# Keys, cached keys, convolution state and parameters in the kernel's own layout in DRAM

## The chip, the cores and the metric

The kernel runs on one core of one Trainium2 chip. The metric is the device time of one execution in microseconds; the time before is the median of three runs. The engines are named as in the profile: PE is TensorE, DVE is VectorE, ACT is ScalarE, POOL is GpSimd, and SP issues most transfers (ACT and POOL can issue transfers too).

## What is computed

The reference is one step of a streaming encoder: one trunk layer over 1024 prompt rows and 32 sample rows, 1056 rows in all, of width 1024. Cut to what matters here:

```
h = rmsnorm(x, g_mix) * (1 + sc1) + sh1          # sc1, sh1, ... from silu(c) @ w_ada + b_ada
u = h @ w_in
qa, ka, va, qm, km, vm, om, ip, fp, ga, gm = split(u)
ya = band_attention(qa, ka, va, rel_bias)        # 8 heads x 64; sample rows also see cache_k, cache_v
new_k, new_v = ka[:, T - keep:], va[:, T - keep:]  # the prompt's last 512 rows; all 32 sample rows
xpad = concatenate([conv_left, concatenate([qm, km])])
conv = sum(xpad[:, j:j + T] * conv_w[j] for j in range(4)) + conv_b
new_conv = xpad[:, -3:]
ym = mlstm(silu(conv), vm, ip, fp, C, n, m)      # 4 heads x 128
merged = sigmoid(ga) * (ya @ w_br_att) + sigmoid(gm) * (ym @ w_br_mlstm)
x = x + gt1 * (merged @ w_out)                   # then a gated feed-forward layer and a last rmsnorm
```

All of it is float32. The new keys and values, the last three rows ahead of the convolution and the mLSTM state are outputs beside y.

## The kernel before, in words

Activations stand with their features on the 128 partitions and the 1056 rows along the free axis, in three tiles of 352 rows. A float32 product is made of three matmuls: each operand is split into a high part (made by ACT) and a low part (made by DVE or POOL), and high x high, low x high and high x low are summed. So a product of 128 output features with a depth of 1024, called a unit, is 8 x 3 = 24 matmuls of 352 columns into one buffer "mm" (`unit`, matmuls at L458). A weight block of 1024 x 128 has three units. SP loads it (`wraw`, L434), ACT and DVE or POOL split it (`wsp`, L424 and L425); `W.advance()` decides when the next ones are loaded and split, in the order of a list.

The program starts with the layer's input, the adaLN products and the norm; then come the first K and V blocks of `w_in`. Attention goes by pairs of heads, `hp` = 0 to 3, each with a K, a V and a Q block. The attention of a pair is made while the products of the next pair run: a generator is stepped by the units. Its steps are scores (psS, L747), bias and maximum (L761 on DVE), exponential (L762 on ACT), normalising (L767 on POOL), transposes of the scores (psT, L774), their split (L781 on ACT, L786 on DVE) and the product with V (psV, L805). In the fourth pair's attention the units beside it are those of the mLSTM's gates and products (L906). The remaining adaLN products run on DVE in between (L1227, L1229), on weights `wa` that SP loads at L1216.

PE transposes whatever has rows on the partitions in DRAM: the small parameters (L239), the cached keys (L700), the convolution state (L860), the keys and the last rows of the convolution on their way out (L582, L587, L1323), and the values (L631), which the kernel itself needs with rows on the partitions. Parameters are loaded by eight transfers into rows of 128 and copied by DVE (L240). After a K block the float32 keys of the last 512 prompt rows and the 32 sample rows stand in `kf` (written by ACT at L571). `k_tail` transposes them in four pieces, ACT copies them (L595) and issues the store itself (L596); `sample_tail` does the same with 32 rows, with a copy by DVE (L589) and a store by SP (L590).

These tails are side work. A K block appends three entries to a list `side.later`: nothing, `k_tail`, `sample_tail`. A V block appends `v_tail` for the first half of the rows, nothing, `v_tail` for the second half, nothing, and `v_sample`, and in the first pair `cache_kv`, which splits the cached keys and values. `unit` takes one entry off this list behind its third, fifth and seventh group of three matmuls. `v_tail` transposes four pieces of the float32 values that ACT copied at L606 and splits them (L619 on ACT, L622 on DVE); the second one also stores them, through L595 and L596.

Every engine works off its instructions in the program's order. A transfer counts its end on one of eight lanes (DMAHW0 to DMAHW7) that are used in turn; an instruction that uses a lane again first waits until the lane's earlier transfer has landed. `q_block` (units of Q) copies each finished unit out of its buffer by ACT (L659, L662).

Of the kernel before, what the change touches and what calls it, by code (L numbers as in the profile page):

```python
# [139 lines left out]
def hybrid_stream_step(  # L140
    ctx: ExitStack,
    tc: tile.TileContext,
    x_prompt, x_sample, cache_k, cache_v, state_conv, state_C, state_n, state_m,
    c_prompt, c_sample, w_ada, b_ada, g_mix, w_in, b_if, conv_w, conv_b, rel_row,
    mh_gain, w_br_att, w_br_mlstm, w_out, g_ffn, w_gate_up, w_down, g_final,
    y_prompt, y_sample, new_k_p, new_v_p, new_conv_p, new_C_p, new_n_p, new_m_p,
# [49 lines left out]
    def f(ap):  # L196
        return ap.bitcast(F32)
# [361 lines left out]
    def k_block(hp):  # L559
        w = w_cols(KA + hp * P)  # L560

        def run():
# [11 lines left out]
            W.advance()  # L574
            side.later += [lambda: None, lambda: k_tail(hp, kf), lambda: sample_tail(kf[:, 512:], new_k_s, hp)]
        run.w = w
        return run

    def k_tail(hp, kf):
        pt = mmt()  # L580
        for i in range(4):
            pe.transpose(pt[:, i * P:(i + 1) * P], kf[:, i * P:(i + 1) * P], ident)  # L582
        put_tokens(pt, new_k_p, hp)

# [102 lines left out]
    def cache_loads():  # L687
        ckv = tmpt((P, 2, 512))
        sp.dma_start(ckv[:, 0], cache_k[0, 0].rearrange("t h d -> t (h d)"))
        sp.dma_start(ckv[:, 1], cache_v[0, 0].rearrange("t h d -> t (h d)"))  # L690
        sp.dma_start(rb_d, bass.AP(rel_row.tensor, rel_row.offset, [[FLEN, H], [0, P], [1, FLEN]]))
        return ckv

    def cache_kv(ckv):
        t = slot([P, 2, 2, 512], F32R)
        cv = t[:, 0].rearrange("p s c -> p (s c)").rearrange("p (h s d) -> p h s d", s=2, d=DH)
        ck = t[:, 1].rearrange("p s (g t) -> p s g t", g=4)
        pt = mmt()
        for g in range(4):
            pe.transpose(pt[:, g * P:(g + 1) * P], ckv[:, 0, g * P:(g + 1) * P], ident)  # L700
# [154 lines left out]
    def conv_state():  # L855
        sp.dma_start(tri[:24], state_conv[0, 0].rearrange("j (r c) -> (j r) c", c=P))

    def mlstm_setup():
        pt = mmt()
        pe.transpose(pt[:, :24], tri[:24], ident[:24, :24])  # L860
        dve.tensor_copy(scol, pt[:, :24])
        pool.memset(tri, 1.0)
# [1372 lines left out]
    for j in range(KD):  # L2235
# [19 lines left out]
        for c, a, b in col_segments(cut, T):  # L2255
# [6 lines left out]


_INS = ["x_prompt", "x_sample", "cache_k", "cache_v", "state_conv", "state_C", "state_n", "state_m",
        "c_prompt", "c_sample", "w_ada", "b_ada", "g_mix", "w_in", "b_if", "conv_w", "conv_b", "rel_bias",
        "mh_gain", "w_br_att", "w_br_mlstm", "w_out", "g_ffn", "w_gate_up", "w_down", "g_final"]
_KV = (1, 1, 512, H, DH)
_OUTS = [(1, S, D), (1, TS, D), _KV, _KV, (1, 1, 3, D), (1, 1, MH, P, P), (1, 1, MH, P), (1, 1, MH),
         (1, 1, TS, H, DH), (1, 1, TS, H, DH), (1, 1, 3, D), (1, 1, MH, P, P), (1, 1, MH, P), (1, 1, MH)]

# [24 lines left out]
```

## Time and profile before

| | us |
|---|---|
| median of three runs | 1608.19 |
| the three runs | 1606.87, 1608.19, 1608.39 |
| the profiled execution's own span | 1604.4 |
| outside the span (median less span) | 3.8 |
| PE busy in the profiled execution | 1576.2 |

The profiled execution has no time of its own but its span, from the first instruction to the last; the runs' times include what lies around it. Rows of the timeline give the start in us from the span's start, the duration, the engine, the line and the operation, what is written and read, how many instructions the row holds, and in brackets the idle time ahead of it with what ended it. A row of PE gives the length of its matmuls with their pipeline, so rows overlap; the starts tell the pace. A wait for several things is put down to the one that came last.

### The profile page before, as it was taken

Reading aid. Unit: us, or ns where it says so; the run is one execution under the profiler, and the core shown is the slowest. Engines: PE = TensorE matmul, PEld = TensorE weight load, DVE = VectorE, ACT = ScalarE, POOL = GpSimd, SP = SyncE. Lnnn points to the kernel's source line nnn. Section 1 sums busy time; section 2 is a strip of 40 time slices with the busy share of each in tenths; the row PEclk is TensorE's granted clock in tenths of the full one; section 3 lists DMA queues with packets and bytes.
Section 4 is the critical chain, followed back from the end, with each engine's and each line's share of the span. In section 5 each row is a group of like instructions: output and inputs, shape, how many; then the busy total and the mean of one; then the engine's idle time right before and its main releaser. Section 6 shows DMA issues by size and latency. Waiting matters only on the chain.

```text
span 1604.4 us, 27406 instructions
## 1 busy us (share of the span) xinstructions
PE 1576.2 (98%) x10256; PEld 1554.8 (97%) x10256; DVE 1135.5 (71%) x2185; ACT 786.2 (49%) x1747; POOL 445.3 (28%) x477
## 2 busy tenths in 40 slices
PE   7999999999999999999999999999999999999997
PEld 6989999999999999999999999999999999999997
DVE  7766564646776855556654699988888986799754
ACT  3665463544455644444443655554544444545443
POOL 2344243433332411000012100566565650000001
PEclk9999999999999999999999999999999999999999
DMA  9823323232222232675353311313222227427453
GB/s 362 273 77 91 97 82 102 88 122 86 67 80 80 69 95 69 121 276 168 121 153 113 106 54 48 100 55 105 81 79 94 67 82 252 135 79 250 135 156 126
DMA packets 210414, 192.45 MB, mean 120 GB/s; under 512 B 10706, under 2 KB 180618, under 8 KB 209258
## 3 DMA queue, kind: packets, MB, share of 16 engines
q1 hardware_dynamic: 205386, 187.82, 37.4%
q10 hardware_dynamic: 4640, 2.82, 0.6%
q8 instruction: 81, 1.33, 0.4%
q14 instruction: 51, 0.42, 0.1%
q0 software_dynamic: 256, 0.06, 0.0%
HBM read 152.19 MB, written 41.63 MB: 121 GB/s over the span
## 4 chain that ended last, share of the span: by engine, by line
PE 88%; DVE 5%; DMA 3%; ACT 2%; issue 1%; SPq 0%; ACTq 0%; POOL 0%; DVEq 0%; POOLq 0%
PE mm L458 39%; PE psb L1843 18%; PE mm L1843 10%; PE mm L2246 3%; PE mm L906 3%; PE psb L2246 2%; PE psV L805 2%; PE psb L2089 2%; PE psS L747 1%; DMA s<-in_w_ada_dram 1%; PE psT L774 1%; PE mm L2089 1%; DMA wraw<-in_w_in_dram 1%; DMA t<-in_x_sample_dram 1%; DVE s L390 1%
## 5 line engine op out<-in xcount | busy, mean ns | idle before, releaser
L458 PE MATMUL mm<-s,wsp 128*128 128x352 f32 x4104 | 689.1, 324 | 0.0
L458 PEld LDWEIGHTS mm<-s,wsp 128*128 128x128 f32 x4104 | 656.9, 188 | 2.0 <-issue 0.4
L425 DVE TENSOR_TENSOR wsp<-wraw,wsp 128x512 fp32r<-128x512 f32 (+1 forms) x280 | 234.9, 855 | 120.0 <-ACT wsp L424 118.0
L1843 PE MATMUL psb<-s,wsp 128*128 128x352 f32 x1611 | 271.7, 322 | 1.5 <-DVE wsp L425 0.8
L424 ACT ACTIVATE wsp<-wraw 128x512 fp32r<-128x512 f32 x336 | 199.5, 617 | 141.5 <-PE psb L1843 44.0
L1843 PEld LDWEIGHTS psb<-s,wsp 128*128 128x128 f32 x1611 | 260.6, 188 | 2.1 <-DVE wsp L425 1.1
L1843 PE MATMUL mm<-s,wsp 128*128 128x352 f32 x933 | 159.3, 322 | 0.0
L1843 PEld LDWEIGHTS mm<-s,wsp 128*128 128x128 f32 x933 | 151.2, 188 | 0.5 <-DVE wsp L425 0.5
L767 POOL TENSOR_SCALAR st<-st,mx 128x640 f32<-128x640 f32 (+5 forms) x72 | 55.7, 774 | 184.8 <-DVE mx L766 170.5
L1229 DVE SCALAR_TENSOR_TENSOR t<-wa,cmix,t 128x512 f32<-128x512 f32 x112 | 89.1, 801 | 15.0 <-DMA wa<-in_w_ada_dram 14.6
L425 POOL TENSOR_TENSOR wsp<-wraw,wsp 128x512 fp32r<-128x512 f32 x56 | 75.8, 1374 | 49.4 <-ACT wsp L424 47.9
L762 ACT ACTIVATE st<-st,mx 128x640 f32<-128x640 f32 (+5 forms) x72 | 47.9, 666 | 71.6 <-DVE mx L761 70.3
L761 DVE CUSTOM_DVE_ANT_0 st<-psS,bias 128x640 f32<-128x640 f32 (+5 forms) x72 | 44.3, 616 | 46.1 <-PE psS L747 33.2
L1790 POOL TENSOR_TENSOR t<-t,sl 128x352 f32<-128x352 f32 x19 | 18.3, 961 | 185.3 <-DMA wraw<-in_w_out_dram 130.8
L781 ACT ACTIVATE pT<-psT 128x640 fp32r<-128x640 f32 (+3 forms) x80 | 38.6, 493 | 63.1 <-PE psT L774 47.7
L2158 POOL TENSOR_TENSOR fst<-fst 128x1 f32<-128x1 f32 (+1 forms) x6 | 1.2, 192 | 236.6 <-ACT t L2151 236.6
L786 DVE TENSOR_TENSOR pT<-psT,pT 128x640 fp32r<-128x640 f32 (+3 forms) x80 | 43.9, 557 | 22.5 <-ACT pT L781 22.3
L1452 POOL TENSOR_TENSOR wraw<-wraw,raw 128x512 f32<-128x512 f32 x33 | 55.8, 1702 | 0.9
L906 PE MATMUL mm<-s,s 128*128 128x264 f32 (+3 forms) x432 | 54.8, 283 | 0.0
L2246 PE MATMUL mm<-s,wsp 128*128 128x352 f32 x330 | 54.4, 324 | 0.0
L2246 PEld LDWEIGHTS mm<-s,wsp 128*128 128x128 f32 x330 | 53.1, 188 | 0.0
L1452 POOL TENSOR_TENSOR spare<-wraw 128x512 f32<-128x512 f32 x11 | 16.5, 1496 | 130.0 <-DMA wraw<-in_w_gate_up_dram 122.4
(396 smaller groups left out, 2561.3 us busy)
## 6 DMA issues: line engine op xcount, KB each, us to landing
wraw<-in_w_in_dram SPq DMA_DIRECT2D x38, 512.0 KB, 4.0
wraw<-in_w_gate_up_dram SPq DMA_DIRECT2D x33, 512.0 KB, 3.8
wa<-in_w_ada_dram SPq DMA_DIRECT2D x64, 256.0 KB, 2.9
wraw<-in_w_down_dram SPq DMA_DIRECT2D x32, 512.0 KB, 4.0
a_d<-t SPq DMA_DIRECT2D x22, 528.0 KB, 2.8
g_d<-t SPq DMA_DIRECT2D x16, 528.0 KB, 3.9
x<-xres SPq DMA_DIRECT2D x16, 528.0 KB, 6.7
t<-g_d SPq DMA_DIRECT2D x16, 528.0 KB, 5.4
```

The lines of the kernel that those rows point to most:

```text
L424: act.activation(dst[:, 0], src, AF.Copy)
L425: eng.tensor_tensor(dst[:, 1], src, f(dst[:, 0]), op=ALU.subtract)
L458: pe.matmul(pt[:, :hi - lo], wt[(w0 + k) // 4][:, a, (w0 + k) % 4], xt[k][:, b, lo:hi], start=(k == 0 and q == 0), stop=(k == n - 1 and q ...
L761: dve.tensor_tensor_reduce(so, sv, bi, -1.0, 3.0e38, ALU.add, ALU.min, mx[:n, 1:2])
L762: act.activation(st[:n, :w], st[:n, :w], AF.Exp, bias=mx[:n, 1:2], scale=-1.0, accum_out=mx[:n, 2:3])
L767: pool.tensor_scalar(st[:n, :w], st[:n, :w], mx[:n, 3:4], 1.0, op0=ALU.mult, op1=ALU.mult)
L906: pe.matmul(pt[:n, :wd], hs[k][:, a, i * P:i * P + n], whl[b][:, k, :wd], start=(k == 0 and q == 0), stop=(k == KD - 1 and q == 2))
L1229: dve.scalar_tensor_tensor(ac[:, c], wa, cmix[:, c, k:k + 1], ac[:, c], op0=ALU.mult, op1=ALU.add)
L1452: self.eng.tensor_tensor(a(dst), a(x), a(y), op=op)
L1843: pe.matmul(acc, wt[:, a, k], x[k][:, b], start=(start and not onto and k == 0 and q == 0), stop=(stop and k == 3 and q == 2), skip_group_ ...
L2089: pe.matmul(acc, wt[k // 4][:, u, k % 4], piece_of[k, i][:, v], start=(k == 0 and q == 0), stop=(k == KP - 1 and q == 2))
L2246: pe.matmul(acc, wt[(k - k0) // 4][:, u, (k - k0) % 4], piece_of[k, 2][:, v], start=(k == 0 and q == 0), stop=(k == NF - 1 and q == 2))
```

## The change

The arrays are brought into the kernel's layout outside the kernel, or left in it: the eight small parameters come as one array `params` of 128 x 124, `cache_k` and `state_conv` come with the features on the partitions, and the new keys and the last rows of the convolution go out with the features on the partitions. The 27 transposes of these by PE, and the copies behind them, go. `v_tail` and `v_sample` stay. The core of the diff:

```diff
-    def param_loads():
-        for row, src in ((R_C, c_prompt), (R_C + 8, c_sample), (R_ADA, b_ada), (R_GMIX, g_mix), (R_GFFN, g_ffn),
-                         (R_GAIN, mh_gain), (R_CB, conv_b)):
-            pool.dma_start(prow[row:row + src.shape[-1] // P], src.rearrange("o (r c) -> (o r) c", c=P))
-        pool.dma_start(prow[R_CW:R_CW + 32], conv_w.rearrange("o j (r c) -> (o j r) c", c=P))
...
-    param_loads()
+    pool.dma_start(cols, params)
...
     def param_cols():
-        pt = ps_v()
-        pe.transpose(pt[:, :NR], prow[:NR], ident[:NR, :NR])
-        dve.tensor_copy(cols, pt[:, :NR])
...
             W.advance()
-            side.later += [lambda: None, lambda: k_tail(hp, kf), lambda: sample_tail(kf[:, 512:], new_k_s, hp)]
+            sp.dma_start(new_k_p[hp], kf[:, :512])
+            sp.dma_start(new_k_s[hp], kf[:, 512:])
...
-    def k_tail(hp, kf):
-        pt = mmt()
-        for i in range(4):
-            pe.transpose(pt[:, i * P:(i + 1) * P], kf[:, i * P:(i + 1) * P], ident)
-        put_tokens(pt, new_k_p, hp)
...
-        sp.dma_start(ckv[:, 0], cache_k[0, 0].rearrange("t h d -> t (h d)"))
+        sp.dma_start(ckv[:, 0], cache_k)
...
-        pt = mmt()
-        for g in range(4):
-            pe.transpose(pt[:, g * P:(g + 1) * P], ckv[:, 0, g * P:(g + 1) * P], ident)
-        pt4 = pt.rearrange("p (g t) -> p g t", g=4)
+        k4 = ckv[:, 0].rearrange("p (g t) -> p g t", g=4)
...
-            act.activation(ck[u, hh], pt4[u], AF.Copy)
+            act.activation(ck[u, hh], k4[u], AF.Copy)
...
-            dve.tensor_tensor(ck[v, hh], pt4[u], f(ck[u, hh]), op=ALU.subtract)
+            dve.tensor_tensor(ck[v, hh], k4[u], f(ck[u, hh]), op=ALU.subtract)
...
-        sp.dma_start(tri[:24], state_conv[0, 0].rearrange("j (r c) -> (j r) c", c=P))
+        sp.dma_start(scol, state_conv)
...
-        pt = mmt()
-        pe.transpose(pt[:, :24], tri[:24], ident[:24, :24])
-        dve.tensor_copy(scol, pt[:, :24])
...
-        pt = mmt()
-        pe.transpose(pt[:48, :P], ncv, ident)
-        ncr = tmpt((48, P))
-        dve.tensor_copy(ncr, pt[:48, :P])
-        sp.dma_start(new_conv_p[0, 0].rearrange("j (r c) -> (j r) c", c=P), ncr[0:24])
-        sp.dma_start(new_conv_s[0, 0].rearrange("j (r c) -> (j r) c", c=P), ncr[24:48])
+        for out, j in ((new_conv_p, 0), (new_conv_s, 3)):
+            sp.dma_start(out, ncv[:, j:j + 3])
```

Line numbers move with the change: L458, L631, L619, L595, L596, L659, L662, L434 and L1216 of the kernel before are L447, L615, L603, L579, L580, L643, L646, L423 and L1194 after. The order of the instructions shows what the shorter list does in the first q block. On PE before: `mm_738`, `mm_783` are the buffers of the first two units, `mm_754` and `mm_768` take the transposed keys, `mm_794` the first V tail.

```order
L458 MATMUL mm_738<-s_531,s_648 128x352 x3
L458 MATMUL mm_738<-s_558,s_648 128x352 x3
L458 MATMUL mm_738<-s_585,s_648 128x352 x3
L582 MATMUL mm_754<-ident,kf_700 128x128 [waits DVE_49,PE_49,Activation_49]
L582 MATMUL mm_754<-ident,kf_700 128x128 [waits Activation_49]
L582 MATMUL mm_754<-ident,kf_700 128x128 x2
L458 MATMUL mm_738<-s_611,s_648 128x352 x3
L458 MATMUL mm_738<-s_638,s_648 128x352 x3
L587 MATMUL mm_768<-ident,kf_700 32x128 [waits DVE_49]
L458 MATMUL mm_738<-s_675,s_648 128x352 x3
```

The same place on PE after: `mm_729` is the first unit, `mm_740` and `mm_759` take the two V tails, and `t_714` holds the values that ACT copies.

```order
L447 MATMUL mm_729<-s_486,s_637 128x352 x3
L447 MATMUL mm_729<-s_520,s_637 128x352 x3
L615 MATMUL mm_740<-ident,t_714 128x128 [waits DVE_49,Activation_49]
L615 MATMUL mm_740<-ident,t_714 128x128
L615 MATMUL mm_740<-ident,t_714 128x128 [waits Activation_49]
L615 MATMUL mm_740<-ident,t_714 128x128
L447 MATMUL mm_729<-s_547,s_637 128x352 x3
L447 MATMUL mm_729<-s_574,s_637 128x352 x3
L447 MATMUL mm_729<-s_600,s_637 128x352 x3
L447 MATMUL mm_729<-s_627,s_637 128x352 x3
L615 MATMUL mm_759<-ident,t_714 128x128 [waits DVE_49]
```

The K tail behind the fifth group and the sample tail behind the seventh are gone; the first V tail has come from the second unit to the first, behind the third group, and the second V tail to the place behind the seventh.

ACT in the same block, before: L595 and L596 copy and store the keys and later the values; L659 and L662 copy the unit `mm_738`, then `mm_783`.

```order
L595 ACTIVATE stg_759<-mm_754 128x512 [waits PE_49]
L596 DMA out_dram<-stg_759 128x4x128 [waits DMAHW4_49,Activation_49]
L659 ACTIVATE t_732<-mm_738 128x352 [waits PE_49]
L662 ACTIVATE s_731<-mm_738 64x352 [waits DVE_49,Pool_49]
L662 ACTIVATE s_731<-mm_738 64x352
L619 ACTIVATE s_793<-mm_794 128x8x64 [waits DMAHW0_49,PE_49]
L619 ACTIVATE s_793<-mm_813 128x8x64 [waits PE_49]
L595 ACTIVATE stg_820<-mm_813 128x512 [waits DMAHW4_49,DVE_49]
L596 DMA out_dram<-stg_820 128x4x128 [waits DMAHW6_49,Activation_49]
L659 ACTIVATE t_732<-mm_783 128x352 [waits PE_49]
```

And after: L603 is the split of the values, L579 and L580 copy and store them, L643 and L646 copy the unit `mm_729`, and L685 splits the cached keys in `t_715`.

```order
L603 ACTIVATE s_739<-mm_740 128x8x64 [waits DVE_49,PE_49,Pool_49]
L603 ACTIVATE s_739<-mm_759 128x8x64 [waits PE_49]
L579 ACTIVATE stg_766<-mm_759 128x512 [waits DVE_49]
L580 DMA out_dram<-stg_766 128x4x128 [waits DMAHW6_49,Activation_49]
L643 ACTIVATE t_723<-mm_729 128x352 [waits PE_49]
L646 ACTIVATE s_722<-mm_729 64x352 [waits DMAHW0_49]
L646 ACTIVATE s_722<-mm_729 64x352
L685 ACTIVATE s_809<-t_715 64x512 [waits DMAHW5_49,DMAHW2_49,DMAHW1_49]
```

The store of the values now stands ahead of the copies of the first unit, where it stood ahead of those of the second. PE's third unit waits for the copies of the first, whose buffer it takes.

The lane that this store waits for, DMAHW6, is held by another transfer, as SP's rows show. Before:

```order
L434 DMA wraw_721<-in_w_in_dram 128x8x128 [waits DMAHW7_49,DMAHW3_49,Pool_49]
L690 DMA t_724<-in_cache_v_dram 128x512 [waits DMAHW5_49]
L1216 DMA wa_733<-in_w_ada_dram 128x512 [waits DMAHW6_49]
L590 DMA out_dram<-stg_770 32x128 [waits DVE_49]
L1216 DMA wa_922<-in_w_ada_dram 128x512 [waits DMAHW0_49]
```

After, with `kf_689` the keys of the first pair:

```order
L423 DMA wraw_710<-in_w_in_dram 128x8x128 [waits DMAHW7_49,DMAHW3_49,Pool_49]
L565 DMA out_dram<-kf_689 128x32 [waits DMAHW4_49]
L673 DMA t_715<-in_cache_k_dram 128x512 [waits DMAHW5_49,PE_49]
L674 DMA t_715<-in_cache_v_dram 128x512 [waits DMAHW6_49]
L1194 DMA wa_724<-in_w_ada_dram 128x512
```

Lane 6 was that of an ada load and is now that of cache_v; cache_k, which stood ahead of the weight load `wraw_721`, now stands behind the same load and behind the sample keys.

In the fourth pair's attention SP's order before was:

```order
L832 DMA ya_d<-t_2920 128x1056 [waits DVE_49]
L678 DMA g_d<-t_3889 128x1056 [waits DMAHW0_49,Activation_49]
L434 DMA wraw_4046<-in_w_in_dram 128x8x128 [waits DMAHW1_49,Pool_49]
L1216 DMA wa_4075<-in_w_ada_dram 128x512 [waits DMAHW4_49,DMAHW2_49,DVE_49]
L1216 DMA wa_4137<-in_w_ada_dram 128x512 [waits DMAHW6_49,DMAHW3_49,DVE_49]
```

And after:

```order
L813 DMA ya_d<-t_2871 128x1056 [waits DVE_49]
L1194 DMA wa_4012<-in_w_ada_dram 128x512 [waits DMAHW4_49,DMAHW0_49,DVE_49]
L662 DMA g_d<-t_3829 128x1056 [waits DMAHW1_49,Activation_49]
L423 DMA wraw_3983<-in_w_in_dram 128x8x128 [waits DMAHW2_49,Pool_49]
L1194 DMA wa_4074<-in_w_ada_dram 128x512 [waits DMAHW6_49,DMAHW3_49,DVE_49]
```

One ada load has moved ahead of a gate store and a weight load. Elsewhere the engines' instructions keep their order, less those that went; the stores of the keys stand on SP ahead of the next weight load (L423), and the two stores of the convolution rows ahead of the ada loads near 560 us.

More of the change, by code (lines that the diff above doesn't have):

```diff
@@ L143, in hybrid_stream_step @@
     x_prompt, x_sample, cache_k, cache_v, state_conv, state_C, state_n, state_m,
-    c_prompt, c_sample, w_ada, b_ada, g_mix, w_in, b_if, conv_w, conv_b, rel_row,
-    mh_gain, w_br_att, w_br_mlstm, w_out, g_ffn, w_gate_up, w_down, g_final,
+    params, w_ada, w_in, b_if, rel_row, w_br_att, w_br_mlstm, w_out, w_gate_up, w_down, g_final,
     y_prompt, y_sample, new_k_p, new_v_p, new_conv_p, new_C_p, new_n_p, new_m_p,
@@ L210, in hybrid_stream_step @@
     pool.memset(ssq, 1.0)
-    prow = tmpt((P, P))
+    NR = R_C + 16
+    cols = cp.tile([P, NR], F32, name="cols")
     xtok = []
-    def param_loads():
-        for row, src in ((R_C, c_prompt), (R_C + 8, c_sample), (R_ADA, b_ada), (R_GMIX, g_mix), (R_GFFN, g_ffn),
-                         (R_GAIN, mh_gain), (R_CB, conv_b)):
-            pool.dma_start(prow[row:row + src.shape[-1] // P], src.rearrange("o (r c) -> (o r) c", c=P))
-        pool.dma_start(prow[R_CW:R_CW + 32], conv_w.rearrange("o j (r c) -> (o j r) c", c=P))
     for i in range(KD):
@@ L226, in hybrid_stream_step @@
         sp.dma_start(xtok[i], xp[i * P:(i + 1) * P])
-    param_loads()
+    pool.dma_start(cols, params)
     xsm = tmpt((TS, D))
     sp.dma_start(xsm, xs_in)
-    NR = R_C + 16
-    cols = cp.tile([P, NR], F32, name="cols")
     csil = cp.tile([P, KD, 2], F32, name="csil")
@@ L2261, in hybrid_stream_step @@
     mm_cm.__exit__(None, None, None)
+_PARAMS = ["b_ada", "g_mix", "g_ffn", "mh_gain", "conv_w", "conv_b", "c_prompt", "c_sample"]
 _INS = ["x_prompt", "x_sample", "cache_k", "cache_v", "state_conv", "state_C", "state_n", "state_m",
[L2265 to L2269, printed above, removed]
+        "params", "w_ada", "w_in", "b_if", "rel_bias",
+        "w_br_att", "w_br_mlstm", "w_out", "w_gate_up", "w_down", "g_final"]
+_V = (1, 1, 512, H, DH)
+_OUTS = [(1, S, D), (1, TS, D), (4, P, 512), _V, (P, 3, KD), (1, 1, MH, P, P), (1, 1, MH, P), (1, 1, MH),
+         (4, P, TS), (1, 1, TS, H, DH), (P, 3, KD), (1, 1, MH, P, P), (1, 1, MH, P), (1, 1, MH)]
 def kernel(**inputs):
@@ L2281 @@
     for name in _INS:
-        a = _np.asarray(inputs[name])
+        if name == "params":
+            a = _np.concatenate([_np.asarray(inputs[n]).reshape(-1, P) for n in _PARAMS]).T
+        else:
+            a = _np.asarray(inputs[name])
         if name == "rel_bias":
             a = _np.pad(a[0][:, ::-1], ((0, 0), (383, 64)), mode="edge")
+        if name == "cache_k":
+            a = a.reshape(P, 4, P).transpose(2, 1, 0).reshape(P, 512)
+        if name == "state_conv":
+            a = a.reshape(24, P).T
         a = _np.ascontiguousarray(a)
@@ L2293 @@
     r = _run(nc, [arrays], core_ids=[0])
-    return tuple(r.results[0][f"out_{i}_dram"] for i in range(len(_OUTS)))
+    outs = [r.results[0][f"out_{i}_dram"] for i in range(len(_OUTS))]
+    for i in (2, 8):
+        outs[i] = _np.ascontiguousarray(outs[i].transpose(2, 0, 1)).reshape(1, 1, -1, H, DH)
+    for i in (4, 10):
+        outs[i] = _np.ascontiguousarray(outs[i].transpose(1, 2, 0)).reshape(1, 1, 3, D)
+    return tuple(outs)
```

## The prediction

> **What bounds the kernel now.** I read the page first, for which engine carries the span.
>
> ```profile
> span 1604.4 us, 27406 instructions
> PE 1576.2 (98%) x10256; PEld 1554.8 (97%) x10256; DVE 1135.5 (71%) x2185; ACT 786.2 (49%) x1747; POOL 445.3 (28%) x477
> PE 88%; DVE 5%; DMA 3%; ACT 2%; issue 1%; SPq 0%; ACTq 0%; POOL 0%; DVEq 0%; POOLq 0%
> ```
>
> PE (TensorE) is busy for 98% of the span, and 88% of the chain that ended last is its own. So a transpose that goes is worth PE's time, unless PE then waits for something else in the same place. The profiled execution's span is 1604.4 us and the median of the runs is 1608.19, so 3.8 us lie around the span; I make the sum as a difference against the span and add it to the median. The runs lie 1.5 us apart, so a change under about 0.2% (3.2 us) can't be told from none.
>
> The longest pieces of the chain of waits, in order of time, show the start and PE's pace.
>
> ```profile
> 4.76 10.22 DMA t<-in_x_sample_dram
> 15.00 20.86 DMA s<-in_w_ada_dram
> ...
> 555.60 22.12 PE mm L458 x138
> ```
>
> Up to 35.86 us the chain is loads. The transposed parameters (one transpose at L239, one copy at L240, eight GpSimd loads) lie under these loads; one load in place of eight brings the same bytes, and I cost this part at nothing. If its cover were gone it could cost one transpose and one copy, about half a microsecond. Undisturbed matmuls of 352 columns start every 22.12/138 = 0.160 us.
>
> **The first q block (68.6 to 83 us).** This is where the order of the work changes most. PE first, then ACT, then SP's issues, all from the timeline.
>
> ```profile
> 68.62 2.65 PE L458 MATMUL mm<-s,s 128*128 128x352 f32 x15
> 71.11 0.60 PE L582 MATMUL mm<-ident,kf 128*128 128x128 f32 x4
> 71.46 1.21 PE L458 MATMUL mm<-s,s 128*128 128x352 f32 x6
> ...
> 81.90 0.66 PE L700 MATMUL mm<-ident,t 128*128 128x128 f32 x4 [0.23 <-ACT s L662]
> ...
> 82.99 1.23 PE L458 MATMUL mm<-s,wsp 128*128 128x352 f32 x6
> ```
> ```profile
> 70.76 1.15 ACT L424 ACTIVATE wsp<-wraw 128x512 fp32r<-128x512 f32 x2 [0.84 <-DMA wraw<-in_w_in_dram]
> 71.82 0.80 ACT L606 ACTIVATE t<-psS 128x352 f32<-128x352 f32 x2
> ...
> 79.09 0.60 ACT L595 ACTIVATE stg<-mm 128x512 f32<-128x512 f32 x1 [0.76 <-DVE s L622]
> 80.12 0.38 ACTq L596 DMA_DIRECT2D out_dram<-stg  x1
> 80.55 0.47 ACT L659 ACTIVATE t<-mm 128x352 f32<-128x352 f32 x1 [0.87 <-DMA wa<-in_w_ada_dram]
> 80.91 0.93 ACT L662 ACTIVATE s<-mm 64x352 fp32r<-64x352 f32 x2
> ```
> ```profile
> 74.04 0.37 SPq L434 DMA_DIRECT2D wraw<-in_w_in_dram  x1
> 74.46 0.66 SPq L690 DMA_DIRECT2D t<-in_cache_v_dram  x1
> 75.17 0.47 SPq L1216 DMA_DIRECT2D wa<-in_w_ada_dram  x1
> ```
>
> The block took 82.99 - 68.62 = 14.37 us for 72 matmuls and its transposes. Four transposes in a row start 71.46 - 71.11 = 0.35 us before the next matmul. Afterwards there are 72 x 0.160 = 11.52 us of matmuls and 0.35 + 0.35 + 0.03 for the V tails and the V sample rows: 12.25.
>
> Two waits are new. The list of side work is three entries shorter, so the first V tail stands behind nine matmuls (68.62 + 1.44 = 70.06), where the K tail stood behind fifteen. It reads the two copies at L606, which end at 71.82 + 0.80 = 72.62, behind ACT's weight split, which had itself waited for a weight load. PE stands there for about 2.5 us. The second wait is behind the V tail's store. ACT issues it itself, and in the order of the instructions it waits for the lane of an earlier transfer. Before, that lane was the ada weight load issued at 75.17: ACT's copy ended at 79.09 + 0.60, and the store went out only at 80.12. Queued behind it were the copies of unit 1 (L659, L662), which ended at 80.91 + 0.93 = 81.84, and PE took its next step at 81.90. Now the lane is that of cache_v, the store is one unit earlier, and queued behind it are the copies of unit 0, whose buffer PE needs for unit 2. Behind 74.04, SP now issues the sample keys, cache_k and then cache_v. So cache_v has a weight load and one transfer of 256 KB ahead of it, as the ada load had. I take 80.0 us for its landing, an estimate from the row at 80.12; then PE starts unit 2 at 80.0 + (81.90 - 80.12) = 81.8. Its own way there is 68.62 + 48 x 0.160 + 0.73 + 2.5 = 79.5, so it waits 2.3 us, and the block ends at 81.8 + 24 x 0.160 = 85.6, which is 2.6 us later than before.
>
> Some of that is given back, since PE waited for the others shortly behind.
>
> ```profile
> 91.61 0.51 PE L747 MATMUL psS<-s,s 128*128 128x256 f32 x2 [0.43 <-DVE mx L761]
> ...
> 97.77 0.41 PE L774 MATMUL psT<-ident,st 128*128 128x128 f32 x2 [0.38 <-DVE pT L786]
> ...
> 103.11 0.52 PE L774 MATMUL psT<-ident,st 128*128 128x128 f32 x3 [0.91 <-POOL wsp L425]
> ```
> ```profile
> 102.55 0.42 DVE L786 TENSOR_TENSOR pT<-psT,pT 128x256 fp32r<-128x256 f32 x1
> ```
>
> A late PE doesn't wait the 0.43 and the 0.38: 2.6 - 0.8 = 1.8. The K tail of the second pair of heads stands just ahead of the wait at 103.11. The profile names POOL there; but the transposes of the scores also wait for the buffer that DVE frees at 102.55 + 0.42 = 102.97. DVE gets there from the last K product, and not sooner for a missing tail, so I count this K tail at 0 (it could be worth its full price, below). ACT and DVE lose a copy each just behind, which I put at 0.1. **Term 1: +1.7 us.** Its ends: if cache_v lands by 77.7 there is no second wait, the block ends at 68.62 + 12.25 + 2.5 = 83.4, 0.4 later, and 0.8 is given back, and perhaps 0.2 more, since ACT and DVE then have less to do: -0.6. If it lands 0.8 later than I take it: +2.5.
>
> **The third and fourth pairs.** The price of a K tail is read where PE doesn't wait.
>
> ```profile
> 185.89 0.60 PE L582 MATMUL mm<-ident,kf 128*128 128x128 f32 x4
> 186.25 1.21 PE L458 MATMUL mm<-s,wsp 128*128 128x352 f32 x6
> 187.30 0.27 PE L587 MATMUL mm<-ident,kf 128*32 128x128 f32 x1
> 187.32 0.73 PE L458 MATMUL mm<-s,wsp 128*128 128x352 f32 x3
> 187.89 0.49 PE L774 MATMUL psT<-ident,st 128*128 128x128 f32 x3
> ```
> ```profile
> 187.04 0.42 DVE L786 TENSOR_TENSOR pT<-psT,pT 128x256 fp32r<-128x256 f32 x1
> ```
> ```profile
> 270.05 0.55 PE L582 MATMUL mm<-ident,kf 128*128 128x128 f32 x3 [0.54 <-ACT kf L571]
> ```
>
> From 185.89 to 187.89 are 2.00 us, of which nine matmuls need 1.44: a K tail costs PE 0.56. [...]
>
> In the third pair PE would now come to 187.89 at 187.33, but DVE frees that buffer at 187.46: 0.4 of the 0.56 is left at most, and a little goes again behind. **Term 2: -0.3** (from -0.56 to -0.1). In the fourth pair PE also waited 0.54 for the float copy of K that only the tail reads: 0.56 + 0.54. **Term 3: -1.1** (to -0.5, if PE then waits for DVE as in the second pair).
>
> **The gates and the rows of the convolution.** In the timeline of PE, and one row of DVE:
>
> ```profile
> 361.74 0.24 PE L860 MATMUL mm<-ident,tri 24*128 24x24 f32 x1
> 361.91 6.10 PE L906 MATMUL mm<-s,s 128*128 128x264 f32 x48
> ...
> 374.10 0.62 PE L747 MATMUL psS<-s,s 128*128 128x384 f32 x2 [0.42 <-DVE mx L761]
> ```
> ```profile
> 372.95 0.75 DVE L1229 SCALAR_TENSOR_TENSOR t<-wa,cmix,t 128x512 f32<-128x512 f32 x1 [2.97 <-DMA wa<-in_w_ada_dram]
> ```
>
> The transpose at L860 is worth 361.91 - 361.74 = 0.17. PE's 0.42 at 374.10 is waited for DVE, which had waited 2.97 for an ada load. On SP that load now stands ahead of a gate store and a weight load that it stood behind, so it comes earlier: -0.4 (0 if it doesn't). **Term 4: -0.6.** The transpose at L1323 lies in a stretch without idle time: **-0.1.** The two narrow stores that take its place are followed on SP by ada loads that nobody on PE waits for there.
>
> Transfers that move: the four K stores go from ACT's queue to SP's, ahead of a weight load that waits for POOL longer than they wait for ACT; I cost this at nothing. If POOL were early, the weight load would stand behind ACT's copy, and the splits that read it behind that.
>
> The sum is +1.7 - 0.3 - 1.1 - 0.6 - 0.1 = -0.4 us: 1608.19 - 0.4 = 1607.8.
>
> **The rivals.** *All PE time counts.* Four K tails (2.24), the cache's four transposes (0.35, as the K tail's four), 0.17 and 0.1 make 2.9; where the waits of 0.23, 0.43, 0.38, 0.54 and 0.42 go too, it is 4.9: 1603.3. For it speaks the page's 98%, and that ACT and DVE lose work in each pair; against it the two new waits on PE and the buffer that holds it at 103.11. It needs cache_v to land by 77.7. [...]
>
> *Slower: narrow rows hold the queue.* The sample keys leave as 128 rows of 128 B, on SP's queue ahead of cache_k and cache_v. From the page's list of DMA issues:
>
> ```profile
> out_dram<-C SPq DMA_DIRECT2D x8, 0.5 KB, 9.2
> Cs<-in_state_n_dram SPq DMA_DIRECT2D x4, 0.5 KB, 3.6
> ```
>
> Transfers of 128 rows of 4 B land after 3.6 us in one case and after 9.2 in another. If the narrow rows add the difference of 5.6 us to cache_v, PE waits as much longer at unit 2: -0.4 + 5.6 = +5.2, 1613.4. Against it: the 9.2 are issued behind larger stores, and may be these stores' time. It is slower at all once cache_v lands after 80.4, and by over 0.2% after 83.6. [...]
>
> *PE waits for the others in every pair.* Then terms 2 and 3 are nothing, as in the second pair: +1.7 - 0.7 = +1.0, 1609.2. For it speaks how close DVE's 187.46 is to PE's 187.33; against it that PE didn't wait in those pairs, but for 0.54 on the tail's own input.
>
> **How the numbers follow.** The forecast has 0.48, all PE time 0.20, narrow rows 0.12, every pair waiting 0.20. Both the forecast and the last rival lie within 0.2%, so no measurable change has 0.68, faster 0.20, slower 0.12. The range reaches down to the ends of the terms (-0.6 - 0.56 - 1.1 - 0.6 - 0.1 = -3.0) and one more for the waits that may go with them, 1604.2; up to +2.5 - 0.1 - 0.5 = +1.9 and one more towards the slower rival, 1611.0.
>
> **What would show it.** In the profile afterwards PE waits at the first V tail (near 70.1, for L606) for 2 to 2.6 us and ahead of unit 2 of the first q block for ACT's copy of unit 0, with the store ahead of that copy issued near 80; the block ends near 85.6. PE's wait near 103 grows. From there on PE is 1.7 us late, and this shrinks to nothing by 375: 0.3 near 188, 1.1 near 270, 0.6 by 375. If the store goes out before 78, or the block ends before 84, term 1 is wrong; if PE is no earlier behind 272 than it was late at 110, terms 2 and 3 are.

## The result, and the profile after

| | before | after |
|---|---|---|
| median of 21 runs each, us | 1607.12 (1606.58 to 1608.39) | 1604.61 (1604.13 to 1605.47) |
| ratio after / before | | 0.9985 [0.9979, 0.9991] |
| span of the profiled execution, us | 1604.4 | 1603.4 |
| PE busy in it, us | 1576.2 | 1574.2 |

The changed kernel is 2.5 us faster, inside the range forecast; the point forecast was 0.4 us faster. Of the 3.2 us between the 1607.8 forecast and 1604.61, 1.1 us belong to no term: the forecast stood on a median of three runs, 1608.19, and the 21 runs have 1607.12. (The transposing outside the kernel is in none of these times.) A later comparison of the same two kernels (below) gave 1604.38 against 1606.25, ratio 0.9988 [0.9979, 0.9997]: 1.9 us. The two profiled executions differ by only 1.0 us, and this is how they go together. In the later comparison the spans of all runs have medians of 1604.2 and 1602.6, so 1.6 us lie in the span; the profiled execution of before is 0.2 over its median, and that of after 0.8. The time less the span is 2.03 us on the mean before and 1.71 after: 0.3 more. 1.6 + 0.3 = 1.9. The other 0.6 of the first comparison is there because both kernels were slower in it, the changed one by 0.2 and the kernel before by 0.9 (1607.12 there, 1606.05 to 1606.25 in all later ones); why is open.

The way to read this change is to compare where the same matmul starts in both traces. PE (TensorE) after, in order of time:

```profile
73.11 1.12 PE L615 MATMUL mm<-ident,t 128*128 128x128 f32 x4 [3.06 <-ACT t L590]
...
82.07 4.11 PE L447 MATMUL mm<-s,s 128*128 128x352 f32 x24 [0.16 <-ACT s L646]
86.02 5.94 PE L447 MATMUL mm<-s,wsp 128*128 128x352 f32 x36
...
104.92 0.52 PE L755 MATMUL psT<-ident,st 128*128 128x128 f32 x3 [1.47 <-POOL wsp L414]
...
189.37 0.52 PE L755 MATMUL psT<-ident,st 128*128 128x128 f32 x3
...
267.38 4.00 PE L447 MATMUL mm<-s,wsp 128*128 128x352 f32 x24
271.22 0.27 PE L755 MATMUL psT<-ident,st 128*128 128x128 f32 x1
...
361.87 5.99 PE L884 MATMUL mm<-s,s 128*128 128x264 f32 x48
...
373.26 0.27 PE L755 MATMUL psT<-ident,st 128*128 128x128 f32 x1
373.28 0.60 PE L728 MATMUL psS<-s,s 128*128 128x384 f32 x2
...
1586.72 7.02 PE L2220 MATMUL mm<-s,wsp 128*128 128x352 f32 x42
```

The rows of before that answer to 267.38, 271.22, 373.26 and 1586.72 (the others stand in the prediction):

```profile
265.86 3.53 PE L458 MATMUL mm<-s,wsp 128*128 128x352 f32 x21
...
270.92 0.27 PE L774 MATMUL psT<-ident,st 128*128 128x128 f32 x1
...
373.40 0.27 PE L774 MATMUL psT<-ident,st 128*128 128x128 f32 x1
...
1587.71 7.02 PE L2246 MATMUL mm<-s,wsp 128*128 128x352 f32 x42
```

After less before: +3.0 at the end of the first q block (86.02 - 82.99), +1.8 at 103, +1.5 at 188, +1.5 at 266, +0.3 at 271, 0.0 at the gates, -0.8 at 374 and -1.0 at 1588. So the change first loses 3 us, then wins 4 back in small steps, and next to nothing happens in the last 1200 us. ACT in the first block shows the loss at its source:

```profile
71.56 1.15 ACT L413 ACTIVATE wsp<-wraw 128x512 fp32r<-128x512 f32 x2 [1.89 <-DMA wraw<-in_w_in_dram]
72.61 0.80 ACT L590 ACTIVATE t<-psS 128x352 f32<-128x352 f32 x2
...
78.81 0.60 ACT L579 ACTIVATE stg<-mm 128x512 f32<-128x512 f32 x1 [0.76 <-DVE s L606]
80.24 0.44 ACTq L580 DMA_DIRECT2D out_dram<-stg  x1
80.73 0.46 ACT L643 ACTIVATE t<-mm 128x352 f32<-128x352 f32 x1 [1.32 <-PE mm L571]
81.09 0.93 ACT L646 ACTIVATE s<-mm 64x352 fp32r<-64x352 f32 x2
```

ACT finished its copy for the store at 78.81 + 0.60 = 79.41 and issued the store at 80.24. The copies of unit 0 behind it ended at 82.02, and PE started unit 2 at 82.07. The row at 80.73 names PE, but the line named (L571) is a transpose that this copy doesn't read; the copy followed the store at once, and the store had 0.8 us to wait. This trace doesn't name what for; by the order of the instructions it is the store's lane, and two of the experiments name it.

### The profile page after: what moved, and what is told of

Same layout as the page of the kernel before. It is cut to its first block, busy times and chain, and to the rows that moved or that the text cites. A ratio compares the mean times of both kernels' runs of the same rounds, so it can differ in the third digit from the quotient of the medians.

```text
span 1603.4 us, 27301 instructions
## 1 busy us (share of the span) xinstructions
PE 1574.2 (98%) x10229; PEld 1554.3 (97%) x10229; DVE 1133.5 (71%) x2178; ACT 784.1 (49%) x1743; POOL 443.0 (28%) x470
## 3 DMA queue, kind: packets, MB, share of 16 engines
q10 hardware_dynamic: 2528, 1.77, 0.4%
## 4 chain that ended last, share of the span: by engine, by line
PE 89%; DMA 4%; DVE 3%; ACT 2%; issue 1%; SPq 0%; POOL 0%; ACTq 0%; DVEq 0%; POOLq 0%
PE mm L447 41%; PE psb L1817 18%; PE mm L1817 10%; PE mm L2220 3%; PE mm L884 3%; PE psb L2220 2%; PE psV L786 2%; PE psb L2063 2%; DMA xres<-s 1%; PE psS L728 1%; DMA s<-in_w_ada_dram 1%; PE psT L755 1%; PE mm L2063 1%; DMA wraw<-in_w_in_dram 1%; DMA s<-in_x_prompt_dram 1%
## 5 line engine op out<-in xcount | busy, mean ns | idle before, releaser
L447 PE MATMUL mm<-s,wsp 128*128 128x352 f32 x4104 | 687.8, 324 | 0.0
L447 PEld LDWEIGHTS mm<-s,wsp 128*128 128x128 f32 x4104 | 657.1, 188 | 1.5 <-issue 0.4
```

The costliest lines, as they stand in the source:

```text
L447: pe.matmul(pt[:, :hi - lo], wt[(w0 + k) // 4][:, a, (w0 + k) % 4], xt[k][:, b, lo:hi], start=(k == 0 and q == 0), stop=(k == n - 1 and q ...
```

## The experiments

The theory after the first trace: the loss in the first q block is made of the two new waits of PE, first V tail and unit 2; the gains behind it are separate. The rivals: the narrow stores of the sample keys delay cache_v; the block's end is set by a chain of other engines, so that waits of PE there are worth nothing; the loss is the clock's. "+x at t" below is the start of the same PE product (transposes left out, the others counted off in order) less that in the trace of before, t being the time in before. The traces already stand apart where the block begins: at 68.5 the changed kernel has -0.25, its second trace +0.28, and the experiments lie between -0.21 and +0.59. What the block itself costs is the step from there. The changed kernel's own trace has +2.92 at 83, +1.74 at 108, +0.23 at 360, -0.83 at 374.5 and -0.99 at 1590.

**The list as long as before.** In `k_block`:

```diff
+            if hp == 0:
+                side.later += [lambda: None] * 3
             sp.dma_start(new_k_p[hp], kf[:, :512])
```

> The changed kernel with three empty entries ahead of the V tails in the first pair, so that the V tails stand where they stood before. Theory A (the advanced V tails make PE wait twice in the first q block, which gives back 1.8 us of what the rest gains): the two waits of PE in that block go, PE is then ahead of the kernel before by about 0.5 us at 111 us instead of 1.8 behind, and the time falls by some 2.3 us below the changed kernel, to about 1602.3 (ratio to before 0.997). Rival B (a delay at this place is taken up behind it by waits that would have been there anyway): the block is shorter in the profile, but the time stays within 0.5 us of the changed kernel's 1604.6.

1602.59 against 1606.2, ratio 0.9977 [0.9967, 0.9986]. PE in this kernel:

```profile
68.51 5.54 PE L447 MATMUL mm<-s,s 128*128 128x352 f32 x33
...
81.52 6.05 PE L447 MATMUL mm<-s,wsp 128*128 128x352 f32 x36 [0.19 <-ACT s L648]
...
91.16 0.51 PE L730 MATMUL psS<-s,s 128*128 128x256 f32 x2 [1.45 <-DVE mx L744]
...
102.66 0.52 PE L757 MATMUL psT<-ident,st 128*128 128x128 f32 x3 [1.47 <-POOL wsp L414]
```

33 matmuls run without a break where the first V tail's wait was, and the block ends 1.47 earlier than before. Both waits hang on the three entries. But PE then waits 1.45 at 91.16 for DVE's maximum, and of the 4.4 us won at 83 (+2.92 to -1.47) only 2.3 are left at 108 (+1.74 to -0.52). In the medians the kernel gains 3.6 us on before, so the entries are worth 1.1 or 1.7 us, as the changed kernel's gain is taken as 2.5 or 1.9; expected were 2.3. The mechanism held, and its size came out smaller.

**The store from SP.** In `put_tokens`:

```diff
-        act.dma_start(out[0, 0]....)
+        (act if hp else sp).dma_start(out[0, 0]....)
```

> The changed kernel with the store of the first pair's values issued by SP instead of ACT, so that ACT's copies of unit 0 don't stand behind a wait for cache_v; the V tails stay advanced. Theory A: PE's first wait (for ACT's copies of V) stays at 2.5 to 3 us, the second one ahead of unit 2 goes (about 2 us in all in that block), PE is near 0 against before at 111 us, and the time is 1.3 to 2 us under the changed kernel: about 1603. Rival B: unchanged at 1604.6. Rival C (the first wait alone carries the cost): the block ends at most 0.5 us earlier.

1602.55, ratio 0.9976 [0.9966, 0.9985].

```profile
72.16 0.79 PE L615 MATMUL mm<-ident,t 128*128 128x128 f32 x4 [1.27 <-ACT t L590]
...
78.09 5.56 PE L447 MATMUL mm<-s,s 128*128 128x352 f32 x33
83.50 5.94 PE L447 MATMUL mm<-s,wsp 128*128 128x352 f32 x36
```

The first wait is still there, at 1.27 us half of what was expected; the second is gone: ACT's copy of unit 0 runs at once, and 33 matmuls pass unit 2 without a break. +0.40 at 83 and -0.78 at 108: the wait that stays is taken up by the waits behind it. So the second wait carries the cost, and it comes from the engine that issues the store, not from the store. (A first wait as long as the 3.06 of the first trace, without the second, was not seen.)

**The keys' outputs alone.** The kernel before, with only the four K blocks' outputs changed:

```diff
-            side.later += [lambda: None, lambda: k_tail(hp, kf), lambda: sample_tail(kf[:, 512:], new_k_s, hp)]
+            sp.dma_start(new_k_p[hp], kf[:, :512])
+            sp.dma_start(new_k_s[hp], kf[:, 512:])
```

> The kernel before with the keys' part of the change alone (K tails gone, SP stores the keys as they stand); parameters, cached keys, state and rows of the convolution as before. Theory A: the same two waits in the first q block, +1.8 us at 111 us against before, then -0.2 in the third pair and -1.4 in the fourth; no gain at the gates (there the ada load stands as before), so about +0.2 in the profile's own alignment and 1606 to 1607.3 in time, some 1 us or more above the changed kernel. Rival D (the K tails carry all of the gain): 1604.6 as the changed kernel.

1608.73, ratio 1.0015 [1.0006, 1.0023]: slower than before. The 27 transposes that went are not what the change is worth: without 20 of them, and with the keys stored by SP as in the change, the kernel takes 2.5 us longer. Expected were 1606 to 1607.3, with +1.8 behind the first block. ACT and PE:

```profile
79.12 0.44 ACTq L597 DMA_DIRECT2D out_dram<-stg  x1
79.61 0.46 ACT L660 ACTIVATE t<-mm 128x352 f32<-128x352 f32 x1 [2.67 <-DMA t<-in_cache_v_dram]
```
```profile
80.95 0.66 PE L701 MATMUL mm<-ident,t 128*128 128x128 f32 x4 [2.01 <-ACT s L663]
81.37 6.15 PE L458 MATMUL mm<-s,s 128*128 128x352 f32 x27
```

Here the profile names the transfer that holds the lane: ACT's copy behind the store waited for cache_v. +3.08 at 108, 1.3 won between 268 and 360, 0.4 lost at the gates (+1.55 at 371, +1.98 at 374.5), +2.00 at 1590. The 27 matmuls at 81.37 should take 27 x 0.160 = 4.3 us, and took 6.15; that is the subject of the last section.

**The parameters alone.** The kernel before with `params` loaded at once and without L239 and L240:

```diff
-    param_loads()
+    pool.dma_start(cols, params)
...
-        pt = ps_v()
-        pe.transpose(pt[:, :NR], prow[:NR], ident[:NR, :NR])
-        dve.tensor_copy(cols, pt[:, :NR])
```

> The kernel before with the parameters' part alone (one array, one load, no transpose, seven inputs less). Theory A (they lie under the first loads): PE aligned with before within 0.3 us from 36 us on, time 1607.1 within 0.5. Rival E (fewer inputs or loads shorten what lies around the span or the start): 1605.6 to 1606.2, which would be the 1.5 us by which the runs gain more than the two traces show.

1606.9, ratio 1.0003 [0.9994, 1.0012]: nothing that can be told from none, as costed, and not the 1605.6 to 1606.2 of the rival. Its products stay within 0.25 us of before up to 360 us and stand 0.67 late at 1590, more than the 0.3 expected. Its time less its span is 1.71 us, like the changed kernel's; the keys alone have 1.89. The median of its spans is 1605.2 against 1604.2, so the span is longer while less lies outside it; why is open.

**The kernel before again.** No edit, for the spread of two traces of one kernel.

> The kernel before, unchanged, for a second trace and for what lies around its span. The changed kernel's runs lie 1.7 us above their own spans, each of 21. If the same holds here (theory F: the profiled execution of before, with its 1604.4, was simply 1.0 us under its median), then the runs of this one lie 1.7 us above their spans and the second trace's span is nearer 1605.4. If 2.7 to 3.8 us lie around the span here (theory G: the change shortens what lies around the span), the seven missing inputs or the shorter start would be worth over 1 us.

1606.05 against 1606.22, ratio 0.9999 [0.999, 1.0009]; from 83 on its products start 0.25 to 0.12 earlier than in the first trace, span 1604.2, time 1606.29. Its times lie 2.04 us over their spans, which is neither theory's figure. The two traces of this kernel agree within 0.3 us, though across the first block they part by 0.4 (+0.18 at 68.5, -0.23 at 83); a smaller step is read only where a second trace repeats it.

**Both edits, list and store.** The first and the second experiment in one kernel.

> The changed kernel with both repairs: the V tails where they stood before, and the first pair's values stored by SP. Theory H (with either repair PE is limited by the chain through ACT and DVE up to 104 us, so what the block gains is waited again at the next scores): no better than either alone, PE 0.5 to 0.8 us ahead of before at 108 us, time as e1 and e2, 0.997 to 0.998 of before. Theory A alone (both savings are PE's own and add up): a further 1.2 us off, 0.9968 or less.

1601.59 against 1606.22, ratio 0.9971 [0.9961, 0.9982], the fastest median of all: its longest run (1602.75) is under the shortest of the changed kernel in the later comparison (1603.25). The profiled execution is that longest run; it loses 1.0 us near 1474, far behind the block.

```profile
81.33 5.94 PE L447 MATMUL mm<-s,wsp 128*128 128x352 f32 x36
...
89.89 0.50 PE L730 MATMUL psS<-s,s 128*128 128x256 f32 x2 [0.48 <-DVE mx L744]
```

PE comes to the scores at 89.89 and waits 0.48, where it waited 1.45 until 91.16 without the second edit. -1.77 at 108 against -0.52 and -0.78 for one edit each. So the theory that a chain of the other engines takes up all that the block gains fell: DVE's maximum, which PE waited for, starts at 89.54 here and at 90.80 without the second edit, so part of that chain stood behind ACT's store. The two gains don't add up either: from 68.5 to 108 the block costs +1.99 in the changed kernel, -0.41 with the list, -1.37 with the store and -1.84 with both. The ratio alone, with its interval, leaves both theories open; it is the traces that decide.

**The convolution state transposed again.** The changed kernel with L860's transpose back, and with it the old place of SP's ada load:

```diff
-        sp.dma_start(scol, state_conv)
+        sp.dma_start(tri[:24], state_conv[0, 0].rearrange("j (r c) -> (j r) c", c=P))
...
+        pt = mmt()
+        pe.transpose(pt[:, :24], tri[:24], ident[:24, :24])
+        dve.tensor_copy(scol, pt[:, :24])
```

> The changed kernel with the convolution state loaded and transposed as before (one transpose, one copy by DVE, and SP's ada load back behind the gate store and the weight load). Theory A: aligned with the changed kernel up to 360 us, then later by 0.2 to 0.4 at the transpose and by another 0.4 to 0.7 at the scores near 374 us, so 0.6 to 1.1 us in all, 1605.2 to 1605.7 where the changed kernel has 1604.6. Rival: a single transpose is 0.2 us, and the ada load's place costs nothing on PE.

1605.72 against 1606.22, ratio 0.9998 [0.9989, 1.0007]. The profiled execution is the slowest of ten (1607.79), so only the step between two points of it is read. PE at the gates:

```profile
363.10 0.24 PE L841 MATMUL mm<-ident,tri 24*128 24x24 f32 x1
363.27 6.10 PE L887 MATMUL mm<-s,s 128*128 128x264 f32 x48
...
375.80 0.62 PE L728 MATMUL psS<-s,s 128*128 128x384 f32 x2 [0.77 <-DVE mx L742]
```

From 360 to 374.5 this kernel goes from +1.36 to +1.71, the changed one from +0.23 to -0.83. So 0.35 lost against 1.06 won: these few edits are worth 1.4 us, more than forecast (0.6) and than expected; the medians say the same (a gain of 1.9 falls to 0.5). The transpose is 363.27 - 363.10 = 0.17 of it. Most of the rest, 1.04, arises at the scores near 374, where PE waits for DVE and DVE for the ada load, which SP issues behind g_d and a weight load again. No run moves the load alone. DVE's step on it waited 2.97 before, 3.31 here, and not at all in the changed kernel:

```profile
374.65 0.75 DVE L1210 SCALAR_TENSOR_TENSOR t<-wa,cmix,t 128x512 f32<-128x512 f32 x1 [3.31 <-DMA wa<-in_w_ada_dram]
```
```profile
361.71 0.33 SPq L1194 DMA_DIRECT2D wa<-in_w_ada_dram  x1
362.56 0.33 SPq L662 DMA_DIRECT2D g_d<-t  x1
```
```profile
371.99 0.92 DVE L1207 SCALAR_TENSOR_TENSOR t<-wa,cmix,t 128x512 f32<-128x512 f32 x1
```

The first of these rows is of this kernel, the others are of the changed one, where the load stands ahead of g_d.

**Narrow rows three times.** Two more stores of the first pair's sample keys, into a buffer that nobody reads:

```diff
+    ks_d = dr.tile([2, P, TS], F32, name="ks_d")
...
             sp.dma_start(new_k_s[hp], kf[:, 512:])
+            if hp == 0:
+                sp.dma_start(ks_d[0], kf[:, 512:])
+                sp.dma_start(ks_d[1], kf[:, 512:])
```

> The changed kernel with the first pair's sample keys stored three times (twice into scratch), all ahead of cache_k and cache_v on SP's queue. Rival of the prediction (narrow rows of 128 B hold the queue, up to 5.6 us each): the ACT store that waits for cache_v goes out as late as 85 to 91 us, and the time rises by 5 us and more. Theory A (a narrow store costs its issue of 0.6 us and about 16 KB): the ACT store goes out 0.8 to 1.5 us later than in the changed kernel, and so does all behind it: 1605.4 to 1606.1.

1604.13 against 1606.22, ratio 0.9988 [0.9978, 0.9997], as without them. SP and ACT:

```profile
73.93 0.57 SPq L566 DMA_DIRECT2D out_dram<-kf  x1
74.55 0.42 SPq L568 DMA_DIRECT2D ks_d<-kf  x1
75.02 0.43 SPq L569 DMA_DIRECT2D ks_d<-kf  x1
...
75.97 0.43 SPq L678 DMA_DIRECT2D t<-in_cache_v_dram  x1
```
```profile
78.88 0.45 ACTq L584 DMA_DIRECT2D out_dram<-stg  x1
79.38 0.46 ACT L647 ACTIVATE t<-mm 128x352 f32<-128x352 f32 x1 [2.42 <-DMA t<-in_cache_v_dram]
```

The store that waits for cache_v went out at 78.88, not later than with one such store (80.24). Each narrow store costs SP about half a microsecond of issue (0.57, 0.42 and 0.43). The rival is dead. Where the profile can name what ACT waits for, it names cache_v: 2.42 of idle time. In this trace the store goes out 2.9 us after cache_v's issue (75.97 to 78.88).

**The changed kernel again.** No edit.

> The changed kernel, unchanged, for a second trace of the first q block. Theory J (the block costs 0.4 us at 108 us where PE's waits in it stay short enough that PE keeps its full clock, and 1.7 to 3 us where a longer wait is followed by some ten matmuls at 0.29 us): this trace shows either of the two at 108 us, with the clock in the rows behind the wait telling which, and the runs lie 2 to 3 us under the kernel before.

Median 1604.38, eleven runs from 1603.25 to 1606.37; the profiled one is that of 1606.37. +4.13 at 83 and +2.95 at 108, 1.2 more than in the first trace of the same kernel. ACT's store, then PE:

```profile
76.72 0.60 ACT L579 ACTIVATE stg<-mm 128x512 f32<-128x512 f32 x1 [0.76 <-DVE s L606]
79.88 0.45 ACTq L580 DMA_DIRECT2D out_dram<-stg  x1
```
```profile
72.16 0.79 PE L615 MATMUL mm<-ident,t 128*128 128x128 f32 x4 [1.57 <-ACT t L590]
...
81.72 5.67 PE L447 MATMUL mm<-s,s 128*128 128x352 f32 x24 [1.90 <-ACT s L646]
87.22 0.96 PE L447 MATMUL mm<-s,wsp 128*128 128x352 f32 x5
```

Here the copy for the store ended at 77.32 and the store went out 2.6 us later. Unit 2 starts 0.35 earlier than in the first trace, but its 24 matmuls took 5.67 us, where they took 4.11: together the 1.2.

**PE kept busy in both waits.** Ten spare matmuls ahead of the first V tail, and ten ahead of unit 2 of the first q block; nobody reads what they write:

```diff
+    def warm(n):
+        pt = ps_v()
+        for i in range(n):
+            pe.matmul(pt[:, :256], hs[0][:, 0, :P], hs[0][:, 0, :256], start=True, stop=True)
     def v_tail(hp, vf, g):
+        if hp == 0 and g == 0:
+            warm(10)
...
             for lo, hi in TILES:
+                if hp == 0 and hi == T:
+                    warm(10)
```

> The changed kernel with ten spare matmuls of 256 columns (about 1.2 us, results unused) ahead of the first V tail and ten ahead of unit 2 of the first q block, the two places where PE waits. Theory J: they lie in the waits, both remaining gaps are under 1.6 us, PE keeps its full clock in the block in every execution, unit 2 runs at 0.16 us a matmul, and the time is the changed kernel's or up to 1 us less, with a smaller spread. Theory K (the slow matmuls come from something else, as the transfers that run then): they are there all the same. If the waits were shorter than the spare work, it would cost up to 2 us.

1604.25 against 1606.25, ratio 0.9987 [0.9977, 0.9996]; runs from 1603.35 to 1605.15.

```profile
79.76 1.34 PE L611 MATMUL psV<-s 128*128 128x256 f32 x10
81.32 4.11 PE L447 MATMUL mm<-s,s 128*128 128x352 f32 x24 [0.22 <-ACT s L654]
```

No matmul of the block is slow, and +0.99 stands at 108 against +1.74 and +2.95, as the theory has it that slow matmuls come behind long waits; the transfers run as before. The median is that of the changed kernel, so the spare matmuls are worth nothing that can be told from none. The runs lie within 1.8 us instead of 3.1, but the changed kernel's first 21 runs lie within 1.4, so the spread proves nothing. Whether the usual execution of the changed kernel meets slow matmuls is not shown: both of its traces do, at different waits, and both are of runs over their medians (1605.10 and 1606.37). The mean clock listed with each run doesn't settle it either: the four longest runs of the later comparison have the lowest, 0.997, but the 21 runs of the first show no such order.

## Why the prediction was partly right

**Term 1, the first q block (+1.7): the mechanism as forecast, the sizes of its waits not.** Forecast were a wait of 2.5 us at the first V tail and one of 2.3 ahead of unit 2, the store at 80.0, unit 2 at 81.8 and the block's end at 85.6. The first trace has 3.06 and 0.16, then 80.24, 82.07 and 86.02; the second has 1.57 and 1.90, then 79.88, 81.72 and 87.22. What held is that the store sets unit 2. In six traces the first V tail is advanced and ACT issues the store: both of the changed kernel, the keys alone, the state transposed, the tripled stores and the spare matmuls. In each of them the step of PE that waits for the copies of unit 0 (unit 2, or with the keys alone the transposes of the cached keys) starts 1.83 or 1.84 us after the store, wherever between 78.88 and 80.24 that goes out; the forecast had 1.78. What did not hold is the first wait. PE's first transposes started 0.50 us behind the start of ACT's first copy (72.61 to 73.11), so they need that one alone and not both, as the forecast read; and the 3.06 of the first trace has its length from ACT's weight split, which waited for its load until 71.56 instead of 70.76.

At 108 the two traces have +1.74 and +2.95. That the first meets the forecast's +1.7 is luck in part: it was 0.25 ahead when the block began, so the block itself cost 1.99, and in the second trace 2.67. For the median execution only what is left over can be told: of the 1.9 us, 2.7 are the later terms (below) and 0.3 lie outside the span, which leaves 2.7 + 0.3 - 1.9 = +1.1, about what the kernel with spare matmuls has without any slow one (+0.99). The step that put both waits into one sum was too simple. With the second wait gone (the store from SP) the first one costs nothing at the end: -0.78 at 108. The second one carries the term: unit 2 starts when the store lets ACT go, whether PE has waited ahead of it or not.

**The second pair's K tail (0): right.** Between 98 and 104 nothing was won (+1.80 at both), and PE's wait near 103 grew from 0.91 to 1.47.

**Term 2 (-0.3): measured -0.15**, from +1.73 at 172 to +1.58 at 200. Of the K tail's 0.56, two thirds and more went again, as argued. Rows of the changed kernel:

```profile
186.17 3.05 PE L447 MATMUL mm<-s,wsp 128*128 128x352 f32 x18
```
```profile
188.80 0.42 DVE L767 TENSOR_TENSOR pT<-psT,pT 128x256 fp32r<-128x256 f32 x1
```

PE's way to the next transposes was 186.17 + 18 x 0.160 = 189.05, DVE freed their buffer at 188.80 + 0.42 = 189.22, and PE started at 189.37.

**Term 3 (-1.1): measured -1.35**, from +1.58 at 200 to +0.23 at 360; 1.2 of it between 268 and 271, where the wait of 0.54 for the keys' float copy went with the tail.

**Term 4 (-0.6): mis-sized, measured -1.06**, from +0.23 to -0.83. The wait went whole, as put, because the ada load comes earlier, as put. But it was sized by the idle time of its row, 0.42, and that is not what it costs: before, the two steps of PE around it start 374.10 - 373.40 = 0.70 apart, after 373.28 - 373.26 = 0.02. The difference of 0.68 is the price; the idle time leaves out the length of the transpose ahead, which otherwise overlaps. The other 0.38 lie ahead of 373, the transpose's 0.17 among them. The last rows of the convolution (-0.1): -0.16. The second trace of the changed kernel repeats all four steps: -0.18, -1.34, -1.06 and -0.09.

**Outside the span: a false step.** The 3.8 us "around the span" set the span of one execution against the median of other ones; the time less the span of the same execution is 2.0 us before and 1.7 after. The 0.3 is nothing that the forecast had. The parameters alone show it too (1.71), so fewer arrays to bind or fewer loads may be its cause; that was not tried, and it can't be all, since the store from SP alone, with the same arrays as the changed kernel, has 1.89. A small slip besides: the range's upper end adds up to 1611.1, not 1611.0.

Term by term, against the 1.9 us of the later comparison: the first block -0.6, the second and third term together -0.1, the gates -0.5, the last rows -0.1, around the span -0.3; -0.4 - 1.6 = -2.0. The sum closes because the first block's +1.1 is what was left over; it shows no more than that no step had the wrong sign.

**The rivals.** All PE time counts: its gain of 4.9 is as far from the 2.5 measured as the forecast's 0.4, and its condition (cache_v by 77.7) didn't hold: in the second trace the store was ready at 77.32 and went out at 79.88. With both waits gone (list and store) the gain is 1606.22 - 1601.59 = 4.6 us, near the 4.9 that this rival sums up. That doesn't prove its sum: some 0.2 of the 4.6 lie outside the span, PE still waits 1.47 near 101, and the store from SP also spares ACT a wait of 0.87 that the kernel before had. Narrow rows: shown wrong by the tripled stores. PE waits for the others in every pair: held in the second pair and nearly in the third, not in the fourth (-1.35). The side "slower" does exist, in the keys' outputs alone (+2.5 us).

## What to carry to other kernels

When work goes from a list that is run beside a stream, everything behind it in the list runs earlier; look at what those entries read, and on which engine's order they then stand. A store waited for the earlier transfer of its lane on the engine that issues it (2.67 and 2.42 us of ACT's idle time in the two traces above that name cache_v), so issue it from an engine whose next instructions nobody needs: here that one line, with three empty entries in the list, raised the gain from 1.9 to 4.6 us (the line alone, to 3.7). Read the gain of a removed instruction in each stage by the starts of the same matmuls in both traces, and take a span and a time from the same execution.

## What the runs showed of the hardware

PE's granted clock fell behind a wait in three traces, in the slowest stretch of 2 us to 0.50 (the keys' outputs alone), 0.52 and 0.56 (the two traces of the changed kernel). The later trace of the changed kernel, stretches of 2 us (the first number behind the five engines is PE's granted clock), unit 2 starting at 81.72:

```profile
82.00:84.00 2.00, 2.00 (x9) 2.00 (x9) 1.87 (x5) 1.93 (x5) 0.83 (x3) 0.59 0.31 88
84.00:86.00 2.00, 2.00 (x9) 2.00 (x9) 1.90 (x4) 0.29 (x1) 1.19 (x2) 0.56 0.00 0
```

In 2 us 9 matmuls pass instead of 12 or more, and slow ones start 0.29 us apart instead of 0.16 (read in the first trace, where they start at 74.61, 74.90, 75.20 and 75.49). By an estimate from these counts about eleven are slow, some 3.2 us; 11 x 0.13 = 1.4 us, most of what lies between 5.67 and 4.11. PE's wait ahead of them was 1.90. In the keys' outputs alone a wait of 2.01 had the same effect (27 matmuls in 6.15 us, the granted clock 0.50 from 82 to 84). In the first trace of the changed kernel it was the wait of 3.06 at 73.11, with a granted clock of 0.52 behind it:

```profile
74.00:76.00 2.00, 2.00 (x9) 2.00 (x8) 0.69 (x1) 0.60 (x1) 1.90 (x3) 0.52 0.07 17
```

There it cost nothing at unit 2, which begins 1.83 us behind the store as in the other traces. From 68 to 82 us ten of the traces (all but the parameters alone and the kernel before again) have four waits of PE over 1.6 us: 1.90, 2.01, 2.09 (the state transposed) and 3.06, and slow matmuls follow each of them; behind the 2.09, 11 matmuls took 2.55 us. The waits between 1.0 and 1.6 us in that stretch, the longest 1.57, are followed by none: 12 matmuls took 2.18 us behind the 1.57.

So one program met the slow stretch at one place in one execution and at another in the next: the changed kernel at 73.11 in its first trace and at 81.72 in its second. Of the waits with slow matmuls behind them, the three of 1.90 to 2.09 us stand 9 to 10 us behind another wait, of 1.18 to 1.57 us. Whether that earlier wait is needed was not tried.
